# End of the second down product: blocks 4 to 7 finished in place on VectorE with one root, half sums as the bias of the root

## The chip, the cores and the metric

The kernel runs on one core of a Trainium2 chip. The metric is the device time of one execution in microseconds (us), the median over the runs of a kernel. In the profile PE is TensorE (PEld its weight loads), DVE is VectorE, ACT is ScalarE, POOL is GpSimd, and SP is the engine whose queue issues the transfers.

## The reference

A trunk of two layers over a sequence of 1024 positions with 1024 channels. Each layer mixes tokens (layer 0 by forgetting attention, layer 1 by a state space mixer, S5), then channels by a dense SwiGLU. Every mixer stands between two RMS norms; the second one's output is added to the residual stream:

```python
def rmsnorm(x, gain):
    xf = x.astype(jnp.float32)
    y = xf * lax.rsqrt(jnp.mean(xf * xf, axis=-1, keepdims=True) + EPS)
    return (y * gain.astype(jnp.float32)).astype(x.dtype)

def swiglu(h, w_gate, w_up, w_down):
    return (jax.nn.silu(h @ w_gate) * (h @ w_up)) @ w_down

...
        x = x + rmsnorm(m, mix_post_gain[i])
        h = rmsnorm(x, ffn_pre_gain[i])
        x = x + rmsnorm(swiglu(h, ffn_w_gate[i], ffn_w_up[i], ffn_w_down[i]), ffn_post_gain[i])
    return x
```

The inner width of the SwiGLU is 2816. The change concerns the last line in layer 1 (the product with `w_down`, its norm, the addition and the store of the result), and, in a smaller part, the line `x + rmsnorm(m, ...)` after the mixers.

## The kernel before, in words

Every fp32 matrix that enters a product is split into a high part h and a low part l (function `split`, L251): ScalarE casts the high part (L253, `gh` for the activations, `wdh` for the weights), VectorE subtracts it (L254, `gl`, `wdl`), and three matmuls (h·h, h·l, l·h) replace one. The program is laid out by a scheduler that fixes one order of instructions per engine; an engine runs its list in order, so that an instruction that waits holds up all behind it. Pages of SBUF are handed out by rings (`R.set`): a name such as `gh` has three pages that are used in turn, and the fourth use waits until all readers of the first are through. Operands are planned in a list (`ffn_plan`) and fetched by `take`, which also splits the operand one ahead and starts the loads of the two behind it; those loads, L231, go through SP's queue.

The sequence is cut into 8 blocks of 128 rows. The down product (`down`, L978) uses one level of a Strassen-like scheme: 11 pairs of inner tiles in each of three phases, one pair being 24 matmuls (two PSUM banks X, Y for each of four blocks), and a last product of 11 inner tiles that is only added to the second halves of blocks 0 to 3. It is done in groups: the pairs j = 0, 1 and 2 one by one (24 matmuls each), then j = 3, 4 and 5 together, 5 inner tiles, block by block: 15 matmuls for block 0, then 15 for block 1, and so on, 60 in all. So each of blocks 0 to 3 is complete after its 15, while blocks 4 to 7 are complete after the third phase (the additions L1023 and L1024 into the buffers `m`).

A complete block goes through `finish`, for layer 1 `fin1` (L1740): y = m · gain, a sum of squares on ScalarE (`rstd`, L290: Square with an accumulator, L296; Sqrt, L300; four small VectorE instructions L302 to L305, one Newton step), x = y · rr + x (L1750), and the store of the block (L1751). The product y is done by GpSimd (L1747), for block 3's second half by VectorE. For blocks 0 to 3 the first half of the row is complete earlier; `begin1` (L1731) is called after group j = 0 and does the first half of y on GpSimd (L1734), the first half's sum of squares (L1735) and the load of x. `rstd` adds the two half sums on VectorE (L298).

The same `rstd` with a half sum serves the last block of each of the two output projections (`after_halves`, L723): y and x there are made in halves, and the first half's sum of squares (L737 for the second norm) is taken before the second half exists.

What the steps touch: `rstd`, `after_halves`, `take`, `down`, `begin1`, `fin1`, and the ring sets ahead of them (L1727).

Of the kernel before, what the change touches and what calls it, by code (L numbers as in the profile page):

```python
# [35 lines left out]
def f32(ap):  # L36
    return ap.bitcast(F32)
# [121 lines left out]
class Trunk:  # L159
    def __init__(self, ctx, tc, A, out):  # L160
        self.tc, self.nc, self.A, self.out = tc, tc.nc, A, out
        nc = self.nc
        mk = lambda name, bufs, **k: ctx.enter_context(tc.tile_pool(name=name, bufs=bufs, **k))
        self.cst = mk("cst", 1)
        self.hp = mk("hp", 4)
        self.pp = mk("pp", 1)
        self.sm = mk("sm", 4)
        self.sq = mk("sq", 1)
        self.ps = mk("ps", 1, space=bass.MemoryType.PSUM).tile([P, 8 * 512], F32, name="ps")
        self.nS, self.slots = 0, (0, 2)  # L170
# [63 lines left out]
    def _cut(self, i):  # L234
        if i < len(self.W) and i == len(self.cut) and self.W[i][4] in self.done:
            self._load(i)
            src, shape, rings = self.W[i][:3]
            raw = self.loaded[i]
            if rings is None:
                self.cut.append(raw)  # L240
                return
            if callable(rings):
                self.cut.append(rings(raw))
            else:
                h, l = self.R(rings[0], shape, F32R), self.R(rings[1], shape, F32R)
# [44 lines left out]
    def rstd(self, src, junk, part=None, out=None):  # L290

        nc = self.nc
        V = nc.vector
        ss = self.small("ss")
        s = slice(0 if part is None else 512, D)
        nc.scalar.activation(junk[:, s], src[:, s], AF.Square, accum_out=ss)  # L296
        if part is not None:
            V.tensor_add(ss, ss, part)  # L298
        rt = self.small("rt")
        self.sqrt = nc.scalar.activation(rt, ss, AF.Sqrt, bias=self.eps, scale=1.0 / D)  # L300
        v, t, rr = self.small("vv"), self.small("tt"), self.small("rr") if out is None else out
        V.tensor_scalar(v, ss, -0.5 / D, -0.5 * EPS, op0=ALU.mult, op1=ALU.add)  # L302
        V.reciprocal(rr, rt)
        V.tensor_scalar(t, v, rr, rr, op0=ALU.mult, op1=ALU.mult)
        V.tensor_scalar(rr, t, 1.5, rr, op0=ALU.add, op1=ALU.mult)  # L305
        return rr

    def norm(self, src, gain, out, pool=False, junk=None):

# [392 lines left out]
    def out_proj(self, xload, gpost, gpre, x_d, order, ops, start):  # L702
# [20 lines left out]
        def after_halves(tb, ps):  # L723
# [4 lines left out]
            sp = self.small("sp")  # L728
            nc.scalar.activation(y[:, lo], ps[:, lo], AF.Square, accum_out=sp)
            yield  # L730
            rr, sp = self.rstd(ps, y, sp), self.small("sp")
            z = R("y")
            for c in (lo, hi):
                stt(y[:, c], ps[:, c], rr, g1[:, c], op0=ALU.mult, op1=ALU.mult)
                nc.vector.tensor_add(x[:, c], x[:, c], y[:, c])
                if c is lo:
                    nc.scalar.activation(z[:, lo], x[:, lo], AF.Square, accum_out=sp)  # L737
# [238 lines left out]
        yield  # L976

    def down(self, finish, begin=lambda tb, m: None, beside=iter(()), steps=((),) * 3, extra=0, last=3,  # L978
             within=lambda tb: None):

# [16 lines left out]
        for ph in range(3):  # L997
            for p in range(n):
# [6 lines left out]
                    mm(Y[tb], g, w, 1, tb, p == 0)  # L1005
                if ph == 0 and p < extra:
                    self.take()
                if p in steps[ph]:
                    with ExitStack() as st:
                        for i in out:  # L1010
                            st.enter_context(self.tc.issue_after(i.ins))
                        next(beside, None)
            with self.tc.high_priority(AHEAD):
                for tb in range(4):
# [6 lines left out]
                    else:  # L1021
                        nc.scalar.copy(b[:, hi], Y[tb])
                        V.tensor_add(b[:, lo], b[:, lo], X[tb])  # L1023
                        V.tensor_add(b[:, hi], b[:, hi], X[tb])  # L1024
        for tb in range(4, 8):
            finish(tb, m[tb])
        js = list(range((n + 1) // 2))
        for i, grp in enumerate([[j] for j in js[:-last]] + [js[-last:]]):
            ops = [(self.take(), self.take()) for j in grp]
            for tb in range(4):  # L1030
                for j, (g, w) in zip(grp, ops):
                    for k in range(min(2, n - 2 * j)):
# [1 line left out]
                if len(grp) > 1:  # L1034
# [545 lines left out]
def trunk(ctx: ExitStack, tc: tile.TileContext, A, out):  # L1580
# [132 lines left out]
    for tb, nx in zip((4, 5, 6, 7, 0, 1, 2, 3), (7, 0, 1, 2, 3)  + (None,) * 3):  # L1713
        next(ins[tb])
        if nx is not None:
# [9 lines left out]
          t1=[29], **EARLY)  # L1725
    gu.send(end)
    R.set(t=[15, 16], gh=[35, 36, 37], gl=[7, 8, 9], wdh=rg(10, 13) + [17],  # L1727
          wdl=[13, 18, 21, 34], m=rg(22, 30), x=[3, 4, 20, 19], y=[5, 6], y4=[5, 6, 15, 16], j=[31], s=[30])
    gp1, part = [], {}

    def begin1(tb, m):  # L1731

        y, sp = R("y4"), T.sq.tile([P, 1], F32, tag=f"sq{tb}", name=T.nm("sq"))
        nc.gpsimd.tensor_mul(y[:, 0:512], m[:, 0:512], gp1[0][:, 0:512])  # L1734
        nc.scalar.activation(R("j")[:, 0:512], m[:, 0:512], AF.Square, accum_out=sp)  # L1735
        x = R("x")
        nc.sync.dma_start(x, x3_d[:, tb, :])
        part[tb] = x, y, sp

    def fin1(tb, m):  # L1740
        if not gp1:
            gp1.append(T.gain("s", A["ffn_post_gain"][1]))
        x, y, sp = part.get(tb) or (R("x"), R("y"), None)
        if sp is None:
            nc.sync.dma_start(x, x3_d[:, tb, :])
        c = slice(0 if sp is None else 512, D)
        (nc.vector if tb == 3 else nc.gpsimd).tensor_mul(y[:, c], m[:, c], gp1[0][:, c])  # L1747
        rr = T.rstd(m, R("j"), sp)
# [34 lines left out]
```

## Time and profile before

| | us |
|---|---|
| runs | 2387.74, 2385.26, 2387.51; median 2387.51 |
| the profiled execution: its own time | 2388.69 |
| its span in the profile | 2386.9 |
| TensorE busy | 2344.8 (98%) |
| VectorE busy | 1684.5 (71%) |
| ScalarE busy | 1198.2 (50%) |
| GpSimd busy | 439.7 (18%) |

The span is what the profile covers, from the first to the last instruction; the execution's own time has 1.8 us more around it. Busy times count an instruction from its start to its end; the ends of matmuls are modelled, so that consecutive ones overlap in the rows. "Idle before" an instruction is the time in which its engine had nothing to do, with the instruction that ended the wait behind an arrow. All times in rows count from the start of the span.

### The profile page before, as it was taken

The numbers are of one execution on the slowest core, as the hardware profiler recorded it, in microseconds if no ns is written. First come the engines' busy times: TensorE is split into PE (matmuls) and PEld (weight loads), VectorE is DVE, ScalarE is ACT, GpSimd is POOL, SyncE is SP. The second block draws the span as 40 slices with busy tenths as digits, with TensorE's granted clock in tenths as the row PEclk, the third lists the DMA queues.
The fourth block names the chain that finished last, engine by engine and source line by source line (L and its number), as shares of the span: only waits on it lengthen the run. The fifth ranks groups of instructions, "written<-read, shape, count | busy, mean of one in ns | idle before, by whom it ended". The sixth has DMA issues, their size and how long they took to land.

```text
span 2386.9 us, 31551 instructions
## 1 busy us (share of the span) xinstructions
PE 2344.8 (98%) x11736; PEld 1945.4 (82%) x11736; DVE 1684.5 (71%) x2680; ACT 1198.2 (50%) x2029; POOL 439.7 (18%) x418
## 2 busy tenths in 40 slices
PE   8999999999999999999999999999999999999998
PEld 6788888888788778888888889888878888888886
DVE  7867787678778966666678785763795655655867
ACT  6766677667645343434554662233463333333444
POOL 3222221222200035555520002410000000000003
PEclk9999999999999999999999999999999999999999
DMA  5121112211443444343698743443434323238874
GB/s 161 36 62 54 54 55 61 63 47 61 138 137 101 120 116 134 122 134 118 202 328 303 270 159 120 132 133 108 130 93 145 109 90 119 96 110 274 286 232 159
DMA packets 256684, 320.61 MB, mean 134 GB/s; under 512 B 34313, under 2 KB 184129, under 8 KB 256530
## 3 DMA queue, kind: packets, MB, share of 16 engines
q1 hardware_dynamic: 256530, 318.59, 41.6%
q8 instruction: 92, 1.51, 0.3%
q14 instruction: 62, 0.51, 0.1%
HBM read 240.82 MB, written 77.72 MB: 133 GB/s over the span
## 4 chain that ended last, share of the span: by engine, by line
PE 79%; DVE 11%; ACT 5%; issue 3%; DMA 2%; POOL 1%; SPq 0%; DVEq 0%; ACTq 0%; POOLq 0%
PE ps L873 30%; PE ps L994 16%; PE ps L272 7%; PE ps L273 7%; PE ps L274 7%; PE ps L634 2%; PE ps L615 2%; PE ps L576 1%; PE ps L577 1%; DVE ps L580 1%; DVE y L319 1%; DVE ptl L619 1%; ACT y L296 1%; POOL o L642 1%; DMA raw<-in_ffn_w_gate_dram 1%
## 5 line engine op out<-in xcount | busy, mean ns | idle before, releaser
L873 PE MATMUL ps<-B,ah 128*128 128x512 f32 x992 | 306.5, 390 | 0.8 <-DVE B L90 0.6
L994 PE MATMUL ps<-wdh,gl 128*128 128x512 f32 x616 | 240.8, 391 | 1.5 <-DVE gl L254 1.5
L994 PE MATMUL ps<-wdh,gh 128*128 128x512 f32 x616 | 241.3, 392 | 0.6 <-DVE s L915 0.6
L994 PE MATMUL ps<-wdl,gh 128*128 128x512 f32 x616 | 241.0, 391 | 0.8 <-DVE wdl L254 0.8
L873 PE MATMUL ps<-ops,ah 128*128 128x512 f32 x704 | 218.9, 392 | 2.4 <-ACT s L930 2.2
L873 PEld LDWEIGHTS ps<-B,ah 128*128 128x128 f32 x992 | 186.1, 188 | 40.9 <-DVE B L90 1.2
L272 PE MATMUL ps<-hT,wh 128*128 128x512 f32 x496 | 197.3, 398 | 0.7 <-DVE pt L455 0.2
L274 PE MATMUL ps<-hT,wl 128*128 128x512 f32 x496 | 194.9, 393 | 0.0
L273 PE MATMUL ps<-hT,wh 128*128 128x512 f32 x496 | 194.5, 392 | 0.0
L873 PE MATMUL ps<-B,al 128*128 128x512 f32 x496 | 193.0, 389 | 0.0
L253 ACT CAST gh<-gr 128x1024 fp32r<-128x1024 f32 (+1 forms) x78 | 81.1, 1040 | 165.2 <-PE ps L994 126.8
L873 PEld LDWEIGHTS ps<-ops,ah 128*128 128x128 f32 x704 | 131.7, 188 | 31.7 <-ACT s L930 2.6
L254 DVE TENSOR_TENSOR gl<-gr,gh 128x1024 fp32r<-128x1024 f32 (+1 forms) x78 | 99.7, 1279 | 76.3 <-ACT gh L253 76.0
L843 DVE TENSOR_TENSOR al<-raw,ah 128x1024 fp32r<-128x1024 f32 x84 | 107.3, 1278 | 55.8 <-ACT ah L842 55.8
L1734 POOL TENSOR_TENSOR y<-m,s 128x512 f32<-128x512 f32 x4 | 6.5, 1628 | 759.7 <-DVE wdl L254 755.0
L619 DVE TENSOR_TENSOR ptl<-ps,pth 128x512 fp32r<-128x512 f32 x192 | 102.5, 551 | 55.2 <-ACT pth L618 54.4
L571 POOL TENSOR_TENSOR An<-An,cmask 128x128 f32<-128x128 f32 x128 | 75.4, 591 | 344.9 <-DVE mx L580 316.4
L994 PEld LDWEIGHTS ps<-wdh,gl 128*128 128x128 f32 x616 | 116.2, 189 | 26.4 <-DVE gl L254 2.6
L994 PEld LDWEIGHTS ps<-wdh,gh 128*128 128x128 f32 x616 | 116.2, 189 | 25.8 <-DVE s L915 1.3
L873 PE MATMUL ps<-ops,al 128*128 128x512 f32 x352 | 137.1, 390 | 0.0
L994 PEld LDWEIGHTS ps<-wdl,gh 128*128 128x128 f32 x616 | 116.3, 189 | 25.4 <-DVE wdl L254 1.2
L842 ACT CAST ah<-raw 128x1024 fp32r<-128x1024 f32 x84 | 88.4, 1052 | 92.9 <-PE ps L873 86.1
(379 smaller groups left out, 5912.3 us busy)
## 6 DMA issues: line engine op xcount, KB each, us to landing
raw<-in_ffn_w_down_dram SPq DMA_DIRECT2D x98, 512.0 KB, 5.3
gr<-g_d SPq DMA_DIRECT2D x76, 512.0 KB, 4.6
raw<-in_ffn_w_gate_dram SPq DMA_DIRECT2D x44, 512.0 KB, 4.1
raw<-in_ffn_w_up_dram SPq DMA_DIRECT2D x44, 512.0 KB, 4.6
g_d<-s SPq DMA_DIRECT2D x66, 256.0 KB, 2.0
raw<-in_fox_w_in_dram SPq DMA_DIRECT2D x32, 512.0 KB, 4.3
g_d<-up SPq DMA_DIRECT2D x44, 256.0 KB, 3.1
g_d<-up SPq DMA_DIRECT2D x21, 512.0 KB, 2.7
```

The source lines that it names most:

```text
L253: self.hcopy(h, src)
L254: self.lsub.tensor_sub(l, src, f32(h))
L272: mm(ps, lh, rh, start=start, stop=False)
L273: mm(ps, lh, rl, start=False, stop=False)
L274: mm(ps, ll, rh, start=False, stop=stop)
L571: nc.gpsimd.tensor_add(An[h][:, qs], An[h][:, qs], self.cmask)
L615: nc.tensor.transpose(p2[:, i], p[:, (g + i) * P:(g + i + 1) * P], self.ident)
L619: nc.vector.tensor_sub(dl, p2[:, 0:n], f32(dh))
L842: nc.scalar.copy(h, src)
L843: V.tensor_sub(l, src, f32(h))
L873: nc.tensor.matmul(bank, x[:, k], y, start=start and k == i == 0, stop=True, skip_group_check=True)
L994: nc.tensor.matmul(bank, x[:, j, t], y[:, j], start=start and i == 0, stop=True, skip_group_check=True)
```

## The change

Four parts.

1. `rstd` with a half sum no longer adds the two sums. A new function `halfsum` takes the first half's sum of squares t0 and makes two small columns from it, t0/D + eps and -0.5·t0/D - 0.5·eps. The first is the bias of the Sqrt, the second the addend in the line for `v`. It is used in `after_halves` and for blocks 0 to 3 here.
2. `begin` is called in the middle of the third phase (phase 2, p = 5) and makes the half sums alone; the gain is fetched there and the Sqrt's table is asked for, behind a split. In `fin1` GpSimd makes the first half of y and VectorE the second, for all four blocks.
3. Blocks 4 to 7 leave `finish`. A new function `rest1`, called once the operands of the last group are taken (with `take(2)`, two ahead), squares the four blocks into four columns, takes one root of 128 x 4, does the Newton step on four columns, and then for each block m = (m · rr) · gain and m = m + x in place, and stores m. Its VectorE instructions are tied behind named splits with `issue_after`.
4. The ring of y becomes four pages; `y4` goes.

```diff
     def split(self, h, l, src):
         with self.tc.high_priority(-100):
-            self.hcopy(h, src)
-            self.lsub.tensor_sub(l, src, f32(h))
+            self.hop = self.hcopy(h, src)
+            self.lop = self.lsub.tensor_sub(l, src, f32(h))
...
         nc.scalar.activation(junk[:, s], src[:, s], AF.Square, accum_out=ss)
-        if part is not None:
-            V.tensor_add(ss, ss, part)
-        rt = self.small("rt")
-        self.sqrt = nc.scalar.activation(rt, ss, AF.Sqrt, bias=self.eps, scale=1.0 / D)
+        rt, (b, h) = self.small("rt"), (self.eps, -0.5 * EPS) if part is None else part
+        self.sqrt = nc.scalar.activation(rt, ss, AF.Sqrt, bias=b, scale=1.0 / D)
         v, t, rr = self.small("vv"), self.small("tt"), self.small("rr") if out is None else out
-        V.tensor_scalar(v, ss, -0.5 / D, -0.5 * EPS, op0=ALU.mult, op1=ALU.add)
+        V.tensor_scalar(v, ss, -0.5 / D, h, op0=ALU.mult, op1=ALU.add)
...
+    def halfsum(self, junk, src, names=None):
+
+        s = slice(0, 512)
+        t = [self.small(f"sp{i}") if names is None else self.sq.tile([P, 1], F32, tag=f"{names}{i}", name=self.nm("sq"))
+             for i in range(3)]
+        self.nc.scalar.activation(junk[:, s], src[:, s], AF.Square, accum_out=t[0])
+        for o, a, b in ((t[1], 1.0 / D, EPS), (t[2], -0.5 / D, -0.5 * EPS)):
+            self.nc.vector.tensor_scalar(o, t[0], a, b, op0=ALU.mult, op1=ALU.add)
+        return t[1:]
...
+                if (ph, p) == (2, n // 2):
+                    for tb in range(4):
+                        begin(tb, m[tb])
...
-        for tb in range(4, 8):
+        for tb in () if behind else range(4, 8):
             finish(tb, m[tb])
         js = list(range((n + 1) // 2))
         for i, grp in enumerate([[j] for j in js[:-last]] + [js[-last:]]):
-            ops = [(self.take(), self.take()) for j in grp]
+            t, a = self.taken, 2 if behind else 1
+            ops = [(self.take(a), self.take(a)) for j in grp]
+            if behind and len(grp) > 1:
+                behind(m, t)
...
     def begin1(tb, m):
 
-        y, sp = R("y4"), T.sq.tile([P, 1], F32, tag=f"sq{tb}", name=T.nm("sq"))
-        nc.gpsimd.tensor_mul(y[:, 0:512], m[:, 0:512], gp1[0][:, 0:512])
-        nc.scalar.activation(R("j")[:, 0:512], m[:, 0:512], AF.Square, accum_out=sp)
-        x = R("x")
-        nc.sync.dma_start(x, x3_d[:, tb, :])
-        part[tb] = x, y, sp
-
-    def fin1(tb, m):
         if not gp1:
             gp1.append(T.gain("s", A["ffn_post_gain"][1]))
...
+            with T.tc.issue_after(T.hop.ins):
+                nc.scalar.preload_act_table_set("sqrt_and_others")
+        part[tb] = T.halfsum(R("j"), m, f"sq{tb}")
+
+    def fin1(tb, m):
+        x, y = R("x"), R("y")
+        nc.sync.dma_start(x, x3_d[:, tb, :])
+        for c in (slice(0, 512), slice(512, D)):
+            (nc.vector if c.start else nc.gpsimd).tensor_mul(y[:, c], m[:, c], gp1[0][:, c])
+        rr = T.rstd(m, R("j"), part[tb])
...
+    def rest1(m, t):
+        V, tbs = nc.vector, range(4, 8)
...
+        with after(-2, dve=False):
+            for i, tb in enumerate(tbs):
+                nc.sync.dma_start(xs[i], x3_d[:, tb, :])
+                nc.scalar.activation(R("j"), m[tb], AF.Square, accum_out=ss[:, i:i + 1])
+            nc.scalar.activation(rt, ss, AF.Sqrt, bias=T.eps, scale=1.0 / D)
+        with after(0):
+            V.tensor_scalar(v, ss, -0.5 / D, -0.5 * EPS, op0=ALU.mult, op1=ALU.add)
+            V.reciprocal(rr, rt)
+            V.tensor_mul(w, rr, rr)
+            V.tensor_mul(w, w, v)
+            V.scalar_tensor_tensor(rr, w, 1.5, rr, op0=ALU.add, op1=ALU.mult)
+        for i, tb in enumerate(tbs):
+            with after(*((0, 1, 3) if i < 2 else (2, 5))):
+                V.scalar_tensor_tensor(m[tb], m[tb], rr[:, i:i + 1], gp1[0], op0=ALU.mult, op1=ALU.mult)
+                V.tensor_add(m[tb], m[tb], xs[i])
+            nc.sync.dma_start(orr[:, tb, :], m[tb])
 
-    T.down(fin1, begin1)
+    T.down(fin1, begin1, behind=rest1)
```

VectorE at the last splits, before: `wdl` and `gl` are the splits of groups j = 3, 4 and 5 (the 512-wide ones are j = 5's), `x` the finished blocks 4 to 7, `rr` and `tt` their roots, `m ... ps` the addition of the last product to block 0.

```order
L254 TENSOR_TENSOR wdl_19629<-raw_19596,wdh_19628 128x1024
L1750 SCALAR_TENSOR_TENSOR x_19456<-y_19457,rr_19467,x_19456 128x1024
L303 RECIPROCAL rr_19485<-rt_19481 128x1
L254 TENSOR_TENSOR gl_19599<-gr_19566,gh_19598 128x1024
L304 TENSOR_SCALAR tt_19484<-vv_19483,rr_19485 128x1
L254 TENSOR_TENSOR wdl_19641<-raw_19632,wdh_19640 128x1024
L305 TENSOR_SCALAR rr_19485<-tt_19484,rr_19485 128x1
L254 TENSOR_TENSOR gl_19635<-gr_19602,gh_19634 128x1024
L1750 SCALAR_TENSOR_TENSOR x_19474<-y_19475,rr_19485,x_19474 128x1024
L254 TENSOR_TENSOR wdl_19651<-raw_19644,wdh_19650 128x512
L254 TENSOR_TENSOR gl_19647<-gr_19638,gh_19646 128x512
L1036 TENSOR_TENSOR m_18075<-m_18075,ps 128x512
```

The same place after the change (from `wdl` of j = 4 and the root on); `m_18083` to `m_18086` are blocks 4 to 7, `s` is the gain.

```order
L1782 SCALAR_TENSOR_TENSOR rs_19602<-rs_19603,rs_19602 128x4
L1785 SCALAR_TENSOR_TENSOR m_18083<-m_18083,rs_19602,s_19213 128x1024
L1785 SCALAR_TENSOR_TENSOR m_18084<-m_18084,rs_19602,s_19213 128x1024
L1786 TENSOR_TENSOR m_18083<-m_18083,x_19595 128x1024
L1786 TENSOR_TENSOR m_18084<-m_18084,x_19596 128x1024
L256 TENSOR_TENSOR gl_19576<-gr_19543,gh_19575 128x1024
L256 TENSOR_TENSOR wdl_19592<-raw_19585,wdh_19591 128x512
L1785 SCALAR_TENSOR_TENSOR m_18085<-m_18085,rs_19602,s_19213 128x1024
L1785 SCALAR_TENSOR_TENSOR m_18086<-m_18086,rs_19602,s_19213 128x1024
L1786 TENSOR_TENSOR m_18085<-m_18085,x_19597 128x1024
L1786 TENSOR_TENSOR m_18086<-m_18086,x_19598 128x1024
L256 TENSOR_TENSOR gl_19588<-gr_19579,gh_19587 128x512
```

All splits up to j = 4's weights now stand ahead of the blocks' own work; blocks 4 and 5 stand ahead of `gl` of j = 4, blocks 6 and 7 between the last `wdl` and the last `gl`.

ScalarE at the end of the second output projection, before (`y ... x` are the two half sums of the last block's second norm, `s` the Silu of the first gate, `rt` the root):

```order
L737 ACTIVATE y_15252,sp_15251<-x_15180 128x512
L296 ACTIVATE y_15252,ss_15259<-x_15180 128x512
L911 ACT_TABLE_LOAD
L911 ACTIVATE s_15288<-s_15288 128x512
L300 ACT_TABLE_LOAD
L300 ACTIVATE rt_15262<-ss_15259,eps 128x1
```

and after:

```order
L313 ACTIVATE y_15260,sp_15263<-x_15186 128x512
L298 ACTIVATE y_15260,ss_15272<-x_15186 128x512
L851 CAST a_1662_15496<-raw_15065 128x512
L300 ACTIVATE rt_15274<-ss_15272,sp_15264 128x1
L920 ACT_TABLE_LOAD
L920 ACTIVATE s_15300<-s_15300 128x512
```

The root now stands ahead of the Silu, and one table load is left of the two here; a third, ahead of the next Silu, goes too.

GpSimd's end, before:

```order
L1747 TENSOR_TENSOR y_19421<-m_18071,s_19418 128x1024
L1747 TENSOR_TENSOR y_19439<-m_18072,s_19418 128x1024
L1747 TENSOR_TENSOR y_19457<-m_18073,s_19418 128x1024
L1747 TENSOR_TENSOR y_19475<-m_18074,s_19418 128x1024
L1734 TENSOR_TENSOR y_2174_19528<-m_18075,s_19418 128x512
L1734 TENSOR_TENSOR y_2177_19535<-m_18076,s_19418 128x512
L1747 TENSOR_TENSOR y_2174_19528<-m_18075,s_19418 128x512
L1747 TENSOR_TENSOR y_2177_19535<-m_18076,s_19418 128x512
L1747 TENSOR_TENSOR y_2180_19542<-m_18077,s_19418 128x512
```

Two halves (blocks 2 and 3) stand ahead of these. After the change the four halves of blocks 0 to 3 are all that is left.

## Rows read from the trace of the kernel before

**Rows 1.** The page's line of engines: busy us, share of the span, instructions.

```profile
PE 2344.8 (98%) x11736; PEld 1945.4 (82%) x11736; DVE 1684.5 (71%) x2680; ACT 1198.2 (50%) x2029; POOL 439.7 (18%) x418
```

**Rows 2.** Timeline of ScalarE: start, us, engine, line, operation, tiles; [idle before <-releaser].

```profile
2331.01 1.05 ACT L253 CAST gh<-gr 128x1024 fp32r<-128x1024 f32 x1 [3.39 <-PE ps L994]
2331.97 1.05 ACT L253 CAST wdh<-raw 128x1024 fp32r<-128x1024 f32 x1
2336.45 1.05 ACT L253 CAST gh<-gr 128x1024 fp32r<-128x1024 f32 x1 [3.43 <-PE ps L994]
...
2343.49 1.06 ACT L296 ACTIVATE j<-m 128x1024 f32<-128x1024 f32 x1
...
2362.97 0.62 ACT L253 CAST gh<-gr 128x512 fp32r<-128x512 f32 x1 [7.38 <-DMA gr<-g_d]
```

**Rows 3.** Timeline of TensorE and its weight loads: the last group's waits, its last matmul.

```profile
2358.60 0.19 PEld L994 LDWEIGHTS ps<-wdh,gl 128*128 128x128 f32 x1 [0.17 <-DVE gl L254]
...
2360.84 0.50 PE L994 MATMUL ps<-wdl,gh 128*128 128x512 f32 x1 [0.81 <-DVE wdl L254]
...
2365.58 0.80 PE L994 MATMUL ps<-wdh,gl 128*128 128x512 f32 x1 [0.72 <-DVE gl L254]
...
2377.65 0.39 PE L994 MATMUL ps<-wdh,gl 128*128 128x512 f32 x1
```

**Rows 4.** Windows of TensorE: stretch, length, busy (matmuls), granted clock, DMA share, GB/s.

```profile
826.00:828.00 2.00, 0.45 (x3) 1.00 0.00 0
828.00:836.00 8.00, 7.88 (x34) 1.00 0.17 55
836.00:840.10 4.10, 0.96 (x3) 1.00 1.16 253
840.20:843.40 3.20, 2.77 (x11) 0.50 1.28 249
...
2362.50:2369.20 6.70, 5.98 (x15) 0.50 0.60 208
```

**Rows 5.** VectorE: groups from 2336 to 2368 (count, busy, mean ns), then timeline.

```profile
L1750 DVE SCALAR_TENSOR_TENSOR x<-y,rr,x 128x1024 f32<-128x1024 f32 x4 | 8.8, 2198 | 0.1
L254 DVE TENSOR_TENSOR wdl<-raw,wdh 128x1024 fp32r<-128x1024 f32 x3 | 5.8, 1941 | 0.0
...
L304 DVE TENSOR_SCALAR tt<-vv,rr 128x1 f32<-128x1 f32 x4 | 1.1, 267 | 0.0
...
2332.10 1.23 DVE L254 TENSOR_TENSOR gl<-gr,gh 128x1024 fp32r<-128x1024 f32 x1 [3.04 <-ACT gh L253]
2333.24 1.22 DVE L254 TENSOR_TENSOR wdl<-raw,wdh 128x1024 fp32r<-128x1024 f32 x1
...
2361.97 1.27 DVE L1750 SCALAR_TENSOR_TENSOR x<-y,rr,x 128x1024 f32<-128x1024 f32 x1
2363.17 0.68 DVE L254 TENSOR_TENSOR wdl<-raw,wdh 128x512 fp32r<-128x512 f32 x1
2363.77 1.75 DVE L254 TENSOR_TENSOR gl<-gr,gh 128x512 fp32r<-128x512 f32 x1
```

**Rows 6.** Timeline of GpSimd: the second early half, and the last 1024-wide product.

```profile
2323.70 1.29 POOL L1734 TENSOR_TENSOR y<-m,s 128x512 f32<-128x512 f32 x1 [4.10 <-DVE wdl L254]
...
2352.77 3.50 POOL L1747 TENSOR_TENSOR y<-m,s 128x1024 f32<-128x1024 f32 x1 [1.16 <-DVE x L1750]
```

**Rows 7.** Timeline of VectorE behind the last matmul: block 3's addition and last stores.

```profile
2378.80 0.68 DVE L1036 TENSOR_TENSOR m<-m,ps 128x512 f32<-128x512 f32 x1
...
2382.45 1.41 DVE L1750 SCALAR_TENSOR_TENSOR x<-y,rr,x 128x512 f32<-128x512 f32 x2
```

**Rows 8.** Output projections: a wait and a table load; a window (PE, PEld, DVE, ACT, POOL).

```profile
1764.44 0.73 PE L873 MATMUL ps<-T,ah 128*128 128x512 f32 x2 [0.26 <-DVE hold L112]
...
1752.18 1.28 ACT L911 ACT_TABLE_LOAD   x1
...
800.00:835.00 35.00, 33.45 (x148) 27.39 (x147) 34.93 (x79) 10.14 (x16) 0.00 (x0) 1.00 0.26 85
```

More of the change, by code (lines that the diff above doesn't have):

```diff
@@ L185, in __init__ @@
         self.W, self.loaded, self.cut, self.taken, self.done = [], [], [], 0, {None}
+        self.ops = {}
     def nm(self, s):
@@ L246, in _cut @@
                 self.split(h, l, raw)
+                self.ops[i] = self.hop.ins, self.lop.ins
                 self.cut.append((h, l))
@@ L727, in after_halves @@
             nc.sync.dma_start(x, xload(tb))
-            sp = self.small("sp")
-            nc.scalar.activation(y[:, lo], ps[:, lo], AF.Square, accum_out=sp)
+            sp = self.halfsum(y, ps)
             yield
-            rr, sp = self.rstd(ps, y, sp), self.small("sp")
+            rr = self.rstd(ps, y, sp)
             z = R("y")
@@ L736, in after_halves @@
                 if c is lo:
-                    nc.scalar.activation(z[:, lo], x[:, lo], AF.Square, accum_out=sp)
+                    sp = self.halfsum(z, x)
             nc.sync.dma_start(x_d[:, tb, :], x)
@@ L978, in down @@
     def down(self, finish, begin=lambda tb, m: None, beside=iter(()), steps=((),) * 3, extra=0, last=3,
-             within=lambda tb: None):
+             within=lambda tb: None, behind=None):
         nc, R = self.nc, self.R
@@ L1038, in down @@
                     within(tb)
-            if i == 0:
-                for tb in range(4):
-                    begin(tb, m[tb])
     def exp(self, x, out, tmp):
@@ L1727, in trunk @@
     R.set(t=[15, 16], gh=[35, 36, 37], gl=[7, 8, 9], wdh=rg(10, 13) + [17],
-          wdl=[13, 18, 21, 34], m=rg(22, 30), x=[3, 4, 20, 19], y=[5, 6], y4=[5, 6, 15, 16], j=[31], s=[30])
+          wdl=[13, 18, 21, 34], m=rg(22, 30), x=[3, 4, 20, 19], y=[5, 6, 15, 16], j=[31], s=[30])
     gp1, part = [], {}
     def begin1(tb, m):
-        y, sp = R("y4"), T.sq.tile([P, 1], F32, tag=f"sq{tb}", name=T.nm("sq"))
-        nc.gpsimd.tensor_mul(y[:, 0:512], m[:, 0:512], gp1[0][:, 0:512])
-        nc.scalar.activation(R("j")[:, 0:512], m[:, 0:512], AF.Square, accum_out=sp)
-        x = R("x")
-        nc.sync.dma_start(x, x3_d[:, tb, :])
-        part[tb] = x, y, sp
-    def fin1(tb, m):
         if not gp1:
             gp1.append(T.gain("s", A["ffn_post_gain"][1]))
[L1743 to L1748, printed above, removed]
+            with T.tc.issue_after(T.hop.ins):
[7 more added lines that the diff above has]
+        rr = T.rstd(m, R("j"), part[tb])
         for s in (slice(0, 512), slice(512, D)) if tb == 3 else (slice(0, D),):
@@ L1751, in fin1, with after @@
             nc.sync.dma_start(orr[:, tb, s], x[:, s])
-    T.down(fin1, begin1)
+    def rest1(m, t):
+        V, tbs = nc.vector, range(4, 8)
+        xs = [R("x") for _ in tbs]
+        ss, rt, v, rr, w = (T.sq.tile([P, 4], F32, tag=f"rs{i}", name=T.nm("rs")) for i in range(5))
+        def after(*items, dve=True):
+            st = ExitStack()
+            for k in items:
+                st.enter_context(T.tc.issue_after(T.ops[t + k][dve]))
+            return st
+        with after(-2, dve=False):
[15 more added lines that the diff above has]
+    T.down(fin1, begin1, behind=rest1)
 _INS = ['x', 'fox_w_in', 'fox_b_f', 'fox_q_gain', 'fox_k_gain', 'fox_w_out', 's5_w_in', 's5_log_dt', 's5_lam_re',
```

## The prediction

> **What bounds the kernel now.** The page's engine line comes first: TensorE is busy 2344.8 of 2386.9 us [rows 1], so a change outside its instructions can only win what TensorE waits for, plus what runs after its last matmul. VectorE at 71% and ScalarE at 50% are not bounds on average, so I read the stretches that the change touches one by one.
>
> Second view: ScalarE's timeline at the end of the second down product. The casts of `gh` come 5.44 us apart [rows 2], one for every 24 matmuls, so a matmul takes 0.227 us while nothing is late. Third: the TensorE instructions with idle time before them [rows 3]. Up to 2358.4 there is none; then the last group of 60 matmuls (blocks 0 to 3, 15 each) waits for `gl`, for `wdl` and twice more for `gl`. Its third matmul starts at 2358.60, 0.17 late; 57 steps of 0.227 later the last one should start at 2371.35, and it starts at 2377.65. So **6.3 us are lost**: about 3 us waiting, the rest because the granted clock stands at 0.50 (1.2 of 2.4 GHz) from 2362.5 to 2369.2 [rows 4]. From the end of the last matmul (2378.04) to the end of the span it is another **8.86 us**. These two numbers are all that the change can reach at the end.
>
> Fourth: why the splits are late. VectorE's groups from 2336 to 2368 show four stores of `x` at 2.20 us and three `wdl` at 1.94, against 1.27 and 1.22 for the same shapes elsewhere, and the last `gl` at 1.75, against 0.68 for a half width [rows 5]: 3.7 + 2.2 + 1.1 = 7.0 us too much, all beside GpSimd's products such as the 3.50 us one at 2352.77 [rows 6].
>
> **The change, part by part.**
>
> *Blocks 4 to 7.* GpSimd's four 1024-wide products go, and seven of its eleven instructions in this stretch with them. VectorE gets back those 7.0 us and pays four additions of 1024 elements, 1.14 each by the step from `gl` to `wdl` [rows 5], 4.6 us; its four stores of `x` become four multiplications into `m` of the same shape, at a step of 1.20 [rows 5]. The balance is 2.4 us, and the order decides what TensorE sees of it.
>
> ScalarE with the order after: `gh` of group j must wait until the matmuls of j-3 have freed its page, so at 2341.9, 2347.3, 2352.8 and 2358.2 for j = 2 to 5 (2336.45 plus multiples of 5.44). Between lie the copies out of PSUM, four Squares at 1.06 and the casts at 0.95 [rows 2]. The fourth Square ends at about 2349.4, the cast of `wdh` 4 at 2350.4, the one root at 2350.7.
>
> VectorE then runs without a gap: `wdl` 4 from 2350.5 to 2351.7; five small instructions on four columns, each needing the one before, 0.9 (an estimate from the single-column `tt`, 0.27 [rows 5]) to 2352.6; two multiplications and two additions, 2 x 1.20 + 2 x 1.14 = 4.7, to 2357.3; `gl` 4 to 2358.4; `wdl` 5 to 2359.0; then four more of those, 4.7, to 2363.7; and only then the half-width `gl` 5, done at **2364.4**. Wanted: `gl` 4 at 2358.43 + 6 x 0.227 = 2359.8 (1.4 us to spare), `gl` 5 at 2358.43 + 12 x 0.227 = **2361.15**. So three of the four waits go, and the fourth grows: TensorE is late by 3.3 us at once. That is what is late next: blocks 6 and 7 now stand on VectorE between `wdl` 5 and `gl` 5. Before, `gl` 5 ended at 2365.5 [rows 5], so it comes only 1.1 us earlier.
>
> After it come 45 matmuls: 10.2 + 0.39, the end at 2375.0 if the clock stays up. Does it? A wait of 1.55 us at 826 to 828 was followed by a clock of 1.00; 3.1 us idle out of 4.1 at 836 to 840 by 0.50 for some 3.4 us, of which the next row shows 3.2 [rows 4]. A wait of 3.3 us is nearest to the second, so I take one such stretch: 3.4 us at half speed cost 1.7, and TensorE ends at 2376.7, against 2378.04: **-1.3 us** (ends: -3.0 with no half-clock stretch, +0.4 with two).
>
> [...]
>
> *Blocks 0 to 3.* The first halves of their sums move to the middle of the third phase, where ScalarE sits idle 3.4 us in every 5.44 [rows 2] and a half Square costs a little over half of 1.06: nothing, and the eight small VectorE instructions too. The same idle time hides the earlier table load (1.28 us by the equal one in [rows 8]); without it the load would delay one `gh`, still two groups ahead of its use. In the last chain the addition of the halves goes; on VectorE the second half of y comes in for blocks 0 to 2 too. Per block 0.60 + 0.60 + 1.20 + some 0.5 of small ones = 2.9 us, less than the 3.4 us that TensorE takes for one, so they do not pile up. After the last matmul: addition from PSUM 0.64, leftovers of block 2 and y 0.9, `vv`, then the store of block 2 to 2.95, then reciprocal, two small ones, and the last store of `x` begins 3.85 after the matmul. Before, it began at 2382.45, 4.4 after, with 4.45 to the end in both [rows 7]: **-0.5 us** (ends 0 and -0.8).
>
> *The queues.* SP's three last `gr` loads now stand ahead of the stores of blocks 4 and 5. Before, the cast of `gh` 5 waited 7.38 us for its `gr` [rows 2]; now that load can go out when `gl` 3 is done, at about 2349.7, and the 7 us row says nothing is left of that wait. The loads of `x` for blocks 2 and 3 go out behind the store of block 7, at about 2364, and are wanted after 2370: nothing. GpSimd keeps four halves that need only early data; one like them ran at 2323.70 [rows 6]: nothing.
>
> *The two output projections.* `rstd` with a bias also serves their last blocks. In the second, the root now stands ahead of the Silu, and two table loads of 1.28 us [rows 8] go; but TensorE waited there only 0.26 us at 1764.44, so I take **-0.2** (ends 0 and -0.5). In the first, VectorE is busy 34.93 of 35 us from 800 to 835 [rows 8], so what is put ahead of an instruction delays it: the `al` that ended the wait at 826 now has one small instruction (0.27 by [rows 5]) more ahead of it, while buffers of S5 come free a little sooner. I take **0** (ends -0.6, two such instructions fewer, and +2.0 if the longer wait at 826 to 828 also brings a half-clock stretch of 1.7).
>
> **Sum:** -1.3 - 0.5 - 0.2 = -2.0 us. The profiled execution took 2388.69 (span 2386.9), 1.18 above the median of the runs; it would become 2386.7. Against the median, 2387.51 - 2.0 = **2385.5 us**. Less than 0.2% (4.8 us) is about what a measurement of this kernel can't tell from no change, so the forecast is: no change.
>
> **The rivals.**
> *The clock stays up* after the wait, as at 826 to 828: 1.7 less, 2383.8. For it: that wait did nothing to the clock; against it: 836 to 840, and 2362 to 2369, where shorter waits did it.
> *No wait at all:* `gl` 5 is in time after all, because the chain on VectorE starts some 3 us before 2350.5. TensorE would win the full 6.3, 2387.51 - 7.0 = 2380.5. Against it: every step of that chain is fixed by the page waits of `gh`.
> *The boundary of the first layer gets worse*, or two half-clock stretches follow: 1.7 to 2.0 more, 2387.2 to 2387.5.
> *Slower:* GpSimd's four remaining halves don't run early but between 2352 and 2364, in the middle of VectorE's chain. Each holds up a VectorE instruction by its 1.29 us, as the stretched rows show [rows 5, 6]: 5.2 us more on `gl` 5, and a second half-clock stretch, 1.7: 2385.5 + 6.9 = 2392.4. It decides if the first of them starts after 2352. The Trainium skill, page "SBUF — State Buffer", section "Who interferes with whom", says of this that the second to come waits for the whole of the first; the rows agree (1.94 for a `wdl`, where 1.22 is usual). Against it: the four need pages that were free, and a gain that was there, when one like them ran at 2323.70 [rows 6].
>
> That the change doesn't do what it says is no case: the order shows each instruction moved.
>
> **How the numbers follow.** Forecast 0.50; clock stays up 0.18; no wait 0.13; worse boundary or two stretches 0.12; slower 0.07. The forecast's own terms spread by some 1 us. Low end: the clock stays up (2383.8), with the low ends of the small terms, about 1.4: 2382.4. High end: 2387.5 with the high ends, 1.4: 2388.9. Outside lie the no-wait case and the slower one, 0.20. Faster by over 0.2% means under 2382.7: the no-wait case and a little of the next, 0.17; slower by over 0.2%, above 2392.3 once runs spread, 0.06; else 0.77.
>
> **What would show it.** Right: no TensorE wait before 2361, then one of about 3.3 us for the half-width `gl`, with the four stores into `m` right ahead of it on VectorE at 1.2 and 1.14; a clock of 0.50 for one stretch after; GpSimd quiet after 2330; last store of `x` 3.9 us after the last matmul. Wrong: a wait under 1 us there, stretched VectorE rows, or a change of more than 2 us before 2336.

## The result, and the profile after

| | before | after |
|---|---|---|
| median, measured with the change (us) | 2388.57 (7 runs) | 2380.13 (7 runs, 2379.55 to 2381.47) |
| ratio, 95% interval | | 0.9964 [0.9952, 0.9975] |
| median, measured a second time (us) | 2388.66 (22 runs) | 2382.01 (10 runs, 2379.66 to 2383.57) |
| ratio, 95% interval | | 0.9971 [0.9962, 0.9981] |
| span of the profile (us) | 2386.9 | 2378.1 |

The change made the kernel 0.3 to 0.4% faster: 8.4 us by the first pair of medians, 6.6 by the second. "No change" at 2385.5 was forecast, with a low end of 2382.4: the first median lies 2.3 below the range, the second 0.4. The 17 runs of the changed kernel together have their median at 2380.97. The page's line of engines after ([rows 1] before):

```profile
PE 2340.3 (98%) x11736; PEld 1942.7 (82%) x11736; DVE 1683.0 (71%) x2684; ACT 1195.2 (50%) x2024; POOL 424.1 (18%) x411
```

**The last group.** TensorE's weight loads and matmuls in the changed kernel: its only wait in this place, and its last matmul ([rows 3] before).

```profile
2361.90 0.19 PEld L1003 LDWEIGHTS ps<-wdh,gl 128*128 128x128 f32 x1 [0.49 <-DVE gl L256]
...
2369.54 0.39 PE L1003 MATMUL ps<-wdh,gl 128*128 128x512 f32 x1
```

Four waits have become one of 0.49 us, and the clock stays up all through. Windows of the changed kernel (columns as in [rows 4], with matmuls, weight loads, VectorE, ScalarE and GpSimd before the granted clock):

```profile
2355.60:2361.90 6.30, 6.23 (x28) 4.84 (x26) 6.25 (x7) 0.62 (x1) 0.00 (x0) 1.00 0.90 328
2361.90:2366.00 4.10, 4.10 (x18) 3.38 (x19) 3.52 (x11) 1.93 (x6) 0.00 (x0) 1.00 0.99 343
2366.00:2369.90 3.90, 3.90 (x18) 2.92 (x16) 3.90 (x8) 1.02 (x3) 0.00 (x0) 1.00 0.54 216
```

VectorE's chain ahead of that wait, in the changed kernel ([rows 5] before):

```profile
2348.16 1.23 DVE L256 TENSOR_TENSOR wdl<-raw,wdh 128x1024 fp32r<-128x1024 f32 x1 [0.69 <-ACT wdh L255]
...
2350.10 2.48 DVE L1785 SCALAR_TENSOR_TENSOR m<-m,rs,s 128x1024 f32<-128x1024 f32 x2
2352.49 2.35 DVE L1786 TENSOR_TENSOR m<-m,x 128x1024 f32<-128x1024 f32 x2
2354.76 1.22 DVE L256 TENSOR_TENSOR gl<-gr,gh 128x1024 fp32r<-128x1024 f32 x1
2355.90 0.68 DVE L256 TENSOR_TENSOR wdl<-raw,wdh 128x512 fp32r<-128x512 f32 x1
2356.50 2.47 DVE L1785 SCALAR_TENSOR_TENSOR m<-m,rs,s 128x1024 f32<-128x1024 f32 x2
2358.89 2.35 DVE L1786 TENSOR_TENSOR m<-m,x 128x1024 f32<-128x1024 f32 x2
2361.16 0.69 DVE L256 TENSOR_TENSOR gl<-gr,gh 128x512 fp32r<-128x512 f32 x1
```

No row is stretched any more, and the order is the forecast one: blocks 6 and 7 stand ahead of the half-width `gl`, which is ready at 2361.85. (All this lies 2.46 us earlier than in the profile of before, as the two casts below show; the forecast 2364.4 less 2.46 is 2361.94.)

**Where the 8.8 us between the two profiles come from.** The same instructions of ScalarE in both kernels, before first:

```profile
820.30 1.05 ACT L842 CAST ah<-S 128x1024 fp32r<-128x1024 f32 x1 [1.96 <-PE ps L873]
872.49 0.63 ACT L911 ACTIVATE s<-s 128x512 f32<-128x512 f32 x1 [3.74 <-DVE s L925]
1499.21 0.37 ACT L1453 ACTIVATE U<-ps,R 128x128 f32<-128x128 f32 x1 [2.66 <-DVE U L1455]
1558.40 1.08 ACT L1412 CAST yT<-ps 128x512 fp32r<-128x512 f32 x2 [0.75 <-PE ps L1408]
```

and after:

```profile
819.65 1.05 ACT L851 CAST ah<-S 128x1024 fp32r<-128x1024 f32 x1 [1.96 <-PE ps L882]
872.40 0.63 ACT L920 ACTIVATE s<-s 128x512 f32<-128x512 f32 x1 [3.73 <-DVE s L934]
1499.10 0.37 ACT L1465 ACTIVATE U<-ps,R 128x128 f32<-128x128 f32 x1 [2.66 <-DVE U L1467]
1556.66 1.07 ACT L1424 CAST yT<-ps 128x512 fp32r<-128x512 f32 x2 [0.75 <-PE ps L1420]
...
2333.99 1.05 ACT L255 CAST gh<-gr 128x1024 fp32r<-128x1024 f32 x1 [3.43 <-PE ps L1003]
```

The last of these stands at 2336.45 in [rows 2]. Read as differences: -0.65 by 820, where TensorE's order is still that of before; +0.56 from 820 to 872; nothing to 1499; -1.63 from 1499 to 1558; -0.72 from there to the cast; then 41.20 us from the cast to the last matmul before (2377.65 - 2336.45) against 35.55 after, **-5.65**; and from the last matmul's start to the end of the span 9.26 (2386.91 - 2377.65) against 8.59 (2378.13 - 2369.54), **-0.67**. The sum is -8.8.

The first and the fourth of these are not the change's: -0.65 is there in full after 100 us, ahead of the first instruction that differs, and from 1000 to 1700 no engine's order differs; what happened at 1540 is the clock, as the windows of before, then of after, around 840 and 1540 show:

```profile
838.00:846.00 8.00, 6.34 (x29) 5.28 (x30) 5.07 (x7) 2.78 (x5) 0.00 (x0) 0.79 0.89 170
1538.00:1545.00 7.00, 6.14 (x39) 6.14 (x40) 7.00 (x15) 1.61 (x2) 2.48 (x3) 0.76 0.88 266
```

```profile
838.00:846.00 8.00, 7.35 (x28) 6.31 (x29) 3.29 (x5) 1.34 (x4) 0.00 (x0) 0.58 0.58 112
1538.00:1545.00 7.00, 6.22 (x47) 5.88 (x48) 7.00 (x15) 2.21 (x3) 2.49 (x3) 1.00 0.86 267
```

In the second profile of the changed kernel (span 2381.7) the same two windows stand at 0.79 and 0.76, as before. So these stretches come and go between executions of one kernel, by some 1.4 us each between these two profiles. The end does not: cast to last matmul took 35.56 us in that second profile. I therefore compare the kernels below by this stretch, **cast to last matmul**, as well as by their medians.

The -0.72 is the second output projection. TensorE's two waits there, before and then after:

```profile
1764.44 0.30 PEld L873 LDWEIGHTS ps<-T,ah 128*128 128x128 f32 x2 [0.68 <-DVE hold L112]
1805.76 0.30 PEld L873 LDWEIGHTS ps<-ops,ah 128*128 128x128 f32 x2 [0.65 <-ACT up L930]
```

```profile
1762.33 0.30 PEld L882 LDWEIGHTS ps<-T,ah 128*128 128x128 f32 x2 [0.25 <-DVE hold L112]
1803.31 0.30 PEld L882 LDWEIGHTS ps<-ops,ah 128*128 128x128 f32 x2 [0.27 <-ACT up L939]
```

They shrink by 0.43 and 0.38.

**What the forecast had missed.** It took the written order of the matmuls for the half-width `gl`. The scheduler's order on TensorE has two differences from before: 17 transposes of the S5 weights stand earlier, at the boundary of the first layer, and one matmul of the last group, `wdh` with the half-width `gl` for block 0, has gone from the 15th place to the 27th. The order of the last group from its 13th matmul, before:

```
wdh,gh (j=5, block 0)
wdl,gh (j=5, block 0)
wdh,gl (j=5, block 0)      <- 15th: first use of the half-width gl
wdh,gh (j=3, block 1)
```

and after:

```
wdh,gh (j=5, block 0)
wdl,gh (j=5, block 0)
wdh,gh (j=3, block 1)
...                        (eleven more of block 1, j=3 and j=4)
wdh,gl (j=5, block 0)      <- 27th
```

The theory to be tested (called the order theory in the expectations): the time won at the end hangs on this one place.

### The profile page after: what moved, and what is told of

It is laid out like the page before. It is cut to its first block, busy times and chain, and to the rows that moved or that the text cites. A ratio compares the mean times of both kernels' runs of the same rounds, so it can differ in the third digit from the quotient of the medians.

```text
span 2378.1 us, 31540 instructions
## 1 busy us (share of the span) xinstructions
PE 2340.3 (98%) x11736; PEld 1942.7 (82%) x11736; DVE 1683.0 (71%) x2684; ACT 1195.2 (50%) x2024; POOL 424.1 (18%) x411
## 4 chain that ended last, share of the span: by engine, by line
PE 80%; DVE 10%; ACT 5%; issue 3%; POOL 1%; DMA 1%; DVEq 0%; SPq 0%; ACTq 0%; POOLq 0%
PE ps L882 32%; PE ps L1003 16%; PE ps L274 7%; PE ps L275 7%; PE ps L276 7%; PE ps L644 2%; PE ps L625 2%; PE ps L586 1%; DVE ps L590 1%; PE ps L587 1%; DVE y L329 1%; DVE ptl L629 1%; ACT y L298 1%; POOL o L652 1%; DMA raw<-in_ffn_w_gate_dram 1%
```

## The experiments

All are timed against the kernel before, and their ratios are to it. They ran in three groups, each on one chip: first the matmul at its written place, gl first, the output projections as before and GpSimd beside the chain; then the changed kernel again, gl first again, the one without ties and the kernel before with VectorE's products; then the one with four roots. "Cast to last matmul" is read from one profile of each kernel.

### The matmul back at its written place

```diff
-            for tb in range(4):
-                for j, (g, w) in zip(grp, ops):
-                    ...
+            for tb in range(4):
+                with self.tc.issue_after(self.lastmm.ins):
+                    for j, (g, w) in zip(grp, ops):
+                        ...
```

TensorE's order is then that of before in this group. `lastmm` is the matmul issued last.

> The changed kernel with one thing taken back: in the last group block 0's last matmul (wdh with the half-width gl) stands at its written place again, the 15th, where the kernel before had it; the changed kernel has it 27th. Order theory (the change won because that matmul was moved behind twelve of block 1's, so that the late gl is wanted 2.7 us later): gl is still ready some 6.3 us after the group's first matmul, and wanted after 14 x 0.227 = 3.2: one TensorE wait of 3.1 us where the changed kernel has 0.49, so +2.6 us against 2380.1, or +4.3 if a half-clock stretch of 3.4 us follows: 2382.7 to 2384.4. Rival (GpSimd's leaving is all that counts, the matmul's place nothing): 2380.1, within 0.5.

Measured: 2384.58 us (11 runs), ratio 0.9984 [0.9976, 0.9993]; cast to last matmul 39.87 us, 4.32 more than in the changed kernel. The cast, TensorE's weight load and last matmul, and windows of the stretch:

```profile
2334.50 1.05 ACT L255 CAST gh<-gr 128x1024 fp32r<-128x1024 f32 x1 [3.43 <-PE ps L1003]
...
2362.39 0.19 PEld L1003 LDWEIGHTS ps<-wdh,gl 128*128 128x128 f32 x1 [3.20 <-DVE gl L256]
...
2374.37 0.39 PE L1003 MATMUL ps<-wdh,gl 128*128 128x512 f32 x1
```

```profile
2359.20:2362.40 3.20, 0.42 (x3) 0.01 (x1) 3.14 (x4) 0.00 (x0) 0.00 (x0) 1.00 0.80 320
2362.40:2364.00 1.60, 1.60 (x7) 1.34 (x8) 1.03 (x2) 0.35 (x1) 0.00 (x0) 0.97 1.06 379
2364.00:2367.40 3.40, 3.40 (x10) 2.63 (x9) 2.50 (x6) 0.67 (x3) 0.00 (x0) 0.51 0.92 317
```

This is the forecast case to the letter: one wait of 3.2 us, then one half-clock stretch of 3.4 us. Against the kernel before, cast to last matmul falls by 41.20 - 39.87 = 1.33 us; the prediction had -1.3. The place of one matmul, then, decides over 4.3 of the 5.65 us: 2.7 us of waiting and the 1.6 that the half-clock stretch costs. By medians it is 4.5 or 2.6 us (against the 2380.13 or the 2382.01 of the changed kernel); whether the clock falls here in every execution, one profile doesn't show.

### The half-width gl ahead of blocks 6 and 7

```diff
-            with after(*((0, 1, 3) if i < 2 else (2, 5))):
+            with after(*((0, 1, 3) if i < 2 else (4, 5))):
```

> The changed kernel with blocks 6 and 7 tied behind the half-width gl instead of ahead of it. VectorE would do that gl right behind the last wdl, some 1.6 us after the group's first matmul; it is wanted after 14 x 0.227 = 3.2 (the matmul stands 15th again here). Order theory: no wait at all, the 0.49 us go: 2379.6; blocks 6 and 7 and block 0's addition end where they did, so nothing is given back. Rival (the stores of blocks 6 and 7, 0.6 us later now, push block 0's chain and the last store): 2380.1 or up to 0.6 above.

Measured: 2380.86 us (6 runs, 2377.30 to 2382.68), ratio 0.9968 [0.9956, 0.9980]; cast to last matmul 35.16 us, 0.39 less than in the changed kernel, and no wait of TensorE. VectorE's row and the window of the last group:

```profile
2356.21 0.68 DVE L256 TENSOR_TENSOR gl<-gr,gh 128x512 fp32r<-128x512 f32 x1
```

```profile
2355.00:2369.00 14.00, 14.00 (x63) 11.46 (x62) 13.94 (x26) 3.69 (x10) 0.00 (x0) 1.00 0.88 317
```

The second time:

> Gl first once more, on the same chip as the changed kernel. Order theory: 0.5 under the changed kernel's median, TensorE again without any wait in the last group. Rival (something is given back behind it): same median or above.

Measured: 2380.77 us (6 runs), ratio 0.9972 [0.9961, 0.9984], beside 2382.01 for the changed kernel in the same group; cast to last matmul 35.16 again. The profiles show the 0.39 us as expected, in both; that the whole is faster than the changed kernel is not shown: over all runs 2380.86 (12) stands against 2380.97 (17), and single runs spread by 7.5 and 4 us. It is the version I would keep, because it needs no late matmul.

### The changed kernel again

> The changed kernel once more, beside the version with gl first and two others, to see what its own runs spread by. Its three half-clock stretches that the change doesn't touch (around 828, 840 and 1540 us) came in some profiles and not in others, 1.0 to 2.0 us each: 2380.1, single runs from 2378 to 2383. If the -8.4 us of the first measurement was partly luck of these, the median comes out up to 1.5 higher.

Measured: 2382.01 us (10 runs), ratio 0.9971 [0.9962, 0.9981], 1.9 above the first median. Part of the first -8.4 may thus be luck, of stretches such as those at 840 and 1540; which executions had them is known for the two profiled ones alone. The end was the same to 0.01 us.

### The output projections as before

```diff
-            sp = self.halfsum(y, ps)
+            sp = self.small("sp")
+            nc.scalar.activation(y[:, lo], ps[:, lo], AF.Square, accum_out=sp)
             yield
-            rr = self.rstd(ps, y, sp)
+            rr, sp = self.rstd(ps, y, sp), self.small("sp")
 ...
-                    sp = self.halfsum(z, x)
+                    nc.scalar.activation(z[:, lo], x[:, lo], AF.Square, accum_out=sp)
```

(`rstd` adds a single half sum as it did before.)

> The changed kernel with the output projections as before: there the two half sums are added again and no half sum enters a bias; the end of the second down product stays changed. If the projections are worth what the two profiles show at their places (TensorE 0.34 us less at the first wait for al, then 0.39 at the second projection's hold and 0.34 at its s): +0.7 to +1.1, 2380.8 to 2381.2. My prediction's term for them was -0.2: 2380.3. If instead the longer half-clock stretch of the changed kernel around 839 to 845 comes from this part, taking it back gains up to 1.0 net: 2379.1.

Measured: 2382.18 us (7 runs), ratio 0.9975 [0.9965, 0.9986]; cast to last matmul 35.55, as in the changed kernel. The two waits of the second projection are back:

```profile
1764.82 0.30 PEld L886 LDWEIGHTS ps<-T,ah 128*128 128x128 f32 x2 [0.74 <-DVE hold L112]
1806.19 0.30 PEld L886 LDWEIGHTS ps<-ops,ah 128*128 128x128 f32 x2 [0.69 <-ACT up L943]
```

0.74 and 0.69 against 0.25 and 0.27: this part is worth some 0.9 us here. In the changed kernel's second profile the two are 0.28 and 0.63, so it is 0.4 to 0.9. What the part does around 840 us is lost in the spread of the clock there.

### GpSimd back beside the chain

```diff
-                V.tensor_add(m[tb], m[tb], xs[i])
+                (nc.gpsimd if i < 2 else V).tensor_add(m[tb], m[tb], xs[i])
```

TensorE's order is held as in the changed kernel, by naming it in the program.

> The changed kernel with the additions of x for blocks 4 and 5 on GpSimd, and TensorE's order held as it is there (the half-width gl wanted 27th). VectorE loses 2 x 1.14 us of work ahead of its gl. Contention theory (GpSimd's instructions stretch VectorE's beside them; 7.0 us in all for four 1024-wide products before): some 1.75 us of stretch for each, 3.5 in all on the stores of blocks 4 to 7 and the two splits, so gl is 1.2 us later and TensorE waits 1.7 instead of 0.49: 2381.3, or 2383.0 with a half-clock stretch. Rival (the stretched rows before had another cause, such as the transfers): VectorE is 2.3 us ahead, no wait, 2379.6.

Measured: 2383.23 us (11 runs), ratio 0.9976 [0.9967, 0.9985]; cast to last matmul 37.66, 2.1 more than in the changed kernel. GpSimd's rows and VectorE's beside them:

```profile
2352.53 3.37 POOL L1800 TENSOR_TENSOR m<-m,x 128x1024 f32<-128x1024 f32 x1 [28.93 <-DVE m L1799]
...
2355.86 3.38 POOL L1800 TENSOR_TENSOR m<-m,x 128x1024 f32<-128x1024 f32 x1
```

```profile
2353.56 3.42 DVE L256 TENSOR_TENSOR gl<-gr,gh 128x1024 fp32r<-128x1024 f32 x1
2356.90 2.89 DVE L256 TENSOR_TENSOR wdl<-raw,wdh 128x512 fp32r<-128x512 f32 x1
```

TensorE's wait for the half-width `gl`, and the window behind it:

```profile
2365.10 0.19 PEld L1005 LDWEIGHTS ps<-wdh,gl 128*128 128x128 f32 x1 [2.40 <-DVE gl L256]
```

```profile
2365.00:2373.00 8.00, 7.89 (x34) 6.31 (x34) 7.38 (x18) 2.94 (x9) 0.00 (x0) 1.00 0.85 306
```

Each of the two splits takes 2.2 us longer than in the changed kernel (1.22 and 0.68). For the two additions taken off VectorE (2.3 us) it pays 4.4, and TensorE waits 0.31 for `wdl` and 2.40 for `gl`. The contention theory holds; its price was 0.45 too low for each. The Trainium skill, page "SBUF — State Buffer", section "Who interferes with whom", says that a VectorE instruction with two inputs from SBUF contends with a GpSimd one that reads SBUF, and that whichever of the two engines comes second waits until the other's instruction is through. The rows agree: `gl` starts at 2353.56, GpSimd's first addition ends at 2355.90, and 2355.90 + 1.1 is where `gl` ends; GpSimd's second starts at 2355.86 and takes as long, which fits a wait for that `gl`.

The clock stayed at 1.00 here, after a wait of 2.40 us, and after the 0.49 of the changed kernel; after the 3.2 us of the kernel with the matmul at its written place it fell.

### Without the ties

```diff
             for k in items:
-                st.enter_context(T.tc.issue_after(T.ops[t + k][dve]))
+                if not dve:
+                    st.enter_context(T.tc.issue_after(T.ops[t + k][dve]))
```

> The changed kernel without the ties of VectorE's instructions behind named splits (those that start ScalarE's squares stay): blocks 6 and 7 come ahead of the full gl of j = 4 as well, which so ends 4.7 us later, some 5.0 us after the group's first matmul; the scheduler then moves its matmuls back on TensorE too, to the 22nd place (wanted 4.8 us after the first), and the half-width gl's to the 28th (wanted 6.1, ready 6.2). Order theory (what counts is where TensorE's order first wants an operand): waits of 0.2 to 0.6 us, 2380.1 within 0.5. By VectorE's order alone, with the matmuls at their written places, TensorE would wait some 3.2 us at the 9th: 2382.8 to 2384.5.

Measured: 2380.75 us (6 runs), ratio 0.9966 [0.9954, 0.9978]; cast to last matmul 35.45. VectorE's full `gl` of j = 4, and the one wait of TensorE:

```profile
2360.34 1.22 DVE L256 TENSOR_TENSOR gl<-gr,gh 128x1024 fp32r<-128x1024 f32 x1
```

```profile
2361.61 0.19 PEld L1003 LDWEIGHTS ps<-wdh,gl 128*128 128x128 f32 x1 [0.41 <-DVE gl L256]
```

That `gl` comes 4.7 us later than in the changed kernel, counted from the cast (25.43 against 20.77), and TensorE loses nothing by it, since its order now wants that `gl` at the 22nd place of the group, not the 9th. The ties are not what gains.

### The kernel before, with the products on VectorE

```diff
-        (nc.vector if tb == 3 else nc.gpsimd).tensor_mul(y[:, c], m[:, c], gp1[0][:, c])
+        (nc.vector if tb >= 3 else nc.gpsimd).tensor_mul(y[:, c], m[:, c], gp1[0][:, c])
```

> The kernel before with one edit: the products of blocks 4 to 7 with the gain on VectorE, not on GpSimd. VectorE loses the 7.0 us of stretched rows and pays four products of about 1.14: 4.6. Contention theory (GpSimd's products were what made the splits late, and the scheduler orders TensorE round what is left): TensorE's loss in the last group falls from 6.3 us to 1 to 2: 2388.0 - 4.8 = 2383.2, within 0.8. Rival (the one root and the work in place are what gains; VectorE is as full with the products): 2386 to 2388.

Measured: 2391.17 us (11 runs), ratio 1.0012 [1.0003, 1.0020]: no gain. Both theories missed. Cast to last matmul took 41.01 us, 0.2 less than before, and from the last matmul's start to the end of the span it was 10.1, 0.9 more. That is 0.7 of the 2.4 us between the two profiles; the other 1.7 were there by the cast, ahead of the first instruction that differs (1.1 of them by one wait at 1184 us, of which the last section has more). So that the edit itself costs 0.1% is not shown. VectorE's rows, and TensorE's wait with the window after it:

```profile
2354.93 1.21 DVE L254 TENSOR_TENSOR gl<-gr,gh 128x1024 fp32r<-128x1024 f32 x1
2356.07 2.28 DVE L1750 SCALAR_TENSOR_TENSOR x<-y,rr,x 128x1024 f32<-128x1024 f32 x1
2358.27 1.21 DVE L254 TENSOR_TENSOR wdl<-raw,wdh 128x1024 fp32r<-128x1024 f32 x1
```

```profile
2359.54 0.19 PEld L994 LDWEIGHTS ps<-wdl,gh 128*128 128x128 f32 x1 [4.37 <-DVE wdl L254]
```

```profile
2359.50:2364.00 4.50, 4.46 (x13) 3.51 (x14) 4.50 (x4) 0.00 (x0) 1.12 (x1) 0.62 1.00 333
```

The four products run at 1.21 to 1.22 here and nothing stretches them, but with the blocks' work called ahead of the last operands, VectorE's order now does all four products and all four stores before the weight split of j = 2, and TensorE waits 4.37 us for that one. Taking GpSimd's products away was not enough by itself; the change also calls the blocks' work behind the operands. GpSimd still has two early halves inside that chain here (as before, where they start at 2357.44 and 2363.32): the first, from 2354.97, runs beside the store of 2.28 us (1.28 alone, so some 1.0 of the wait); the second, from 2358.43, runs beside the next `gl`, which takes 2.29.

### Four roots in place of one

```diff
-                nc.scalar.activation(R("j"), m[tb], AF.Square, accum_out=ss[:, i:i + 1])
-            nc.scalar.activation(rt, ss, AF.Sqrt, bias=T.eps, scale=1.0 / D)
-        with after(0):
-            ...
+                rrs.append(T.rstd(m[tb], R("j")))
 ...
-                V.scalar_tensor_tensor(m[tb], m[tb], rr[:, i:i + 1], gp1[0], op0=ALU.mult, op1=ALU.mult)
+                V.scalar_tensor_tensor(m[tb], m[tb], rrs[i], gp1[0], op0=ALU.mult, op1=ALU.mult)
```

> The changed kernel with a root and a chain of four one-column instructions for each of blocks 4 to 7 in place of one root of 128 x 4; the work in place, its place behind the splits and the ties stay. Order theory: the extra small instructions of the first blocks fill VectorE's idle time before the last full weight split, gl is ready at the same place (wanted one matmul later, 28th), so the last group takes what it takes in the changed kernel (22.8 us from the matmul at 2349 of the kernel before to the last one) within 0.3, and the whole about 2381. Rival (the single root is what saved VectorE the time: three chains of 0.9 us fewer): gl 2 to 3 us later, a wait of 2.5 us or more, 2383 to 2385.

Measured: 2380.94 us (7 runs), ratio 0.9970 [0.9958, 0.9981]; cast to last matmul 35.43 (the changed kernel's 35.55 is the 22.8 of the expectation, counted from a later point). Its only wait there:

```profile
2362.99 0.19 PEld L1003 LDWEIGHTS ps<-wdh,gl 128*128 128x128 f32 x1 [0.39 <-DVE gl L256]
```

The single root gains nothing that this stretch shows: three more roots and eleven more small instructions don't lengthen it.

## Why the prediction was wrong

*What bounds the kernel, and the two numbers at the end.* Right: 6.3 us lost in the last group and the chain after it were where most of the time came from.

*Blocks 4 to 7 on VectorE.* Right. Counted back by 2.46 us, the root's chain was forecast to begin behind `wdl` 4 at 2349.2 (2349.39 measured, 2348.16 + 1.23), `gl` 4 to be ready at 2355.9 (2355.98), `gl` 5 at 2361.94 (2361.85). The stretched rows went with GpSimd, as said.

*"Wanted: `gl` 5 at 2358.43 + 12 x 0.227 = 2361.15."* **This step failed.** That is the 15th matmul, its place before. In the changed kernel it is the 27th, so it is wanted 12 x 0.227 = 2.7 us later, at 2363.9 in the time of before, and `gl` 5, ready at 2364.4, is 0.5 late, not 3.3 (0.49 measured). I had read the new order of VectorE, ScalarE and GpSimd, and for TensorE taken the old one; "the order shows each instruction moved" was said without the engine that the whole sum is about. With the right place the same sum has 0.5 lost of 6.3, -5.8, and with the other two terms -6.5, where the runs have -6.6 and -8.4. (That 2387.5 - 6.5 = 2381.0 meets the 2380.97 of the 17 runs is luck: the base, a median of three runs, was 1.1 under the medians of before that were measured with the change.) Two of the prediction's own signs of being wrong came: the wait under 1 us, and a change of more than 2 us ahead of 2336, which was 2.46, 1.6 of it the clock at 1540.

*The half-clock stretch.* Right as a price: where the wait of 3.2 us was brought back, one stretch of 3.4 us at 0.51 followed. As it didn't come to that wait, the stretch went as well, 1.6 us more.

*The rivals.* The time of "no wait at all", 2380.5, was the nearest, and its reason was wrong: VectorE's chain did not begin 3 us sooner, TensorE's use came later. Its chance of 0.13 was argued from VectorE alone. That GpSimd's early halves could run inside the chain did not happen in the changed kernel, where the last two of the four start at 2315.80 and 2321.24; in the kernel with the products on VectorE two of them did.

*The tail, -0.5.* Nearly right, 0.67: block 3's last store begins 3.73 us after the last matmul's end (3.85 forecast); the additions and the last store in the changed kernel ([rows 7] before):

```profile
2369.97 0.69 DVE L1051 TENSOR_TENSOR m<-m,ps 128x512 f32<-128x512 f32 x1
...
2373.66 1.42 DVE L1758 SCALAR_TENSOR_TENSOR x<-y,rr,x 128x512 f32<-128x512 f32 x2
```

*The output projections, -0.2 and 0.* Too small for the second: 0.4 to 0.9. I had looked at the wait of 0.26 that the matmul's row shows; the weight load's row shows 0.68 at the same place, and the wait at 1805 had not been looked at. For the first, nothing that rises over the spread of the clock there.

## What to carry to other kernels

Where a scheduler sets the order, an operand's due time is where the *new* order first uses it: compare the order of the waiting engine too, not only of the engine that makes the operand. Here one matmul put behind twelve others was worth 4.3 of the 5.65 us won in this stretch. And work moved off a shared engine must also be called late enough: here, moved to VectorE but left ahead of the splits, it gained nothing.

## What the runs showed that was not expected

The two profiles of the changed kernel differ by 1.1 to 1.5 us at each of four places, with the same instructions: at 840 and 1540, as shown, and from 601 to 605, by the granted clock (1.00 in the first, 0.57 in the second), but also at 1184, where the clock stays at 1.00 and one wait for VectorE's `s` takes 1.02 us in one and 2.12 in the other. The end part, in contrast, took 35.55 and 35.56 us, and 35.16 twice. As long as no such place lies in it, a part's time in two profiles shows a difference under a microsecond, as here the 0.39, which medians of some ten runs do not show.

Of two waits the shorter left the clock alone: 2.40 us at full speed after, 3.20 us with 1.6 us of full clock behind it and then 3.4 us at 0.51. The length of a single wait does not sort them, though: in the kernel before, the longest single wait of a weight load between 2345 and 2362.5 was 1.25 us (at 2360.84), and the clock fell to 0.50 [rows 4]. What decides is open.
